# Layer 0 of a hybrid decoder: the first queries, keys and values taken step by step together, with the gates and the norm among the last steps

## The chip, the cores and the metric

One core of one Trainium2 chip runs the whole program. The time is the device time of one execution in microseconds (us); the kernel before has a median of 1263.06 us over three runs. TensorE (PE) does the matrix products, VectorE (DVE) and ScalarE (ACT) the elementwise work, GpSimd (POOL) a part of the weight preparation, and SyncE (SP) issues most of the transfers.

## The reference, cut to what matters

Two layers work on 528 tokens (16 learned ones and 512 real ones) of width 1024. A layer normalises its input, makes one combined projection, runs two groups of heads on it and adds the result back; a gated feed-forward block follows.

```
xn = rmsnorm(h, attn_norm_g)
proj = einsum('bld,dc->blc', xn, w_in)
fq, fk, fv, flog, rq, rk, rv, rg = split(proj)
logf = log_sigmoid(flog + b_fgate)              # 8 forget gates
c = cumsum(logf)                                # along the tokens
logit[t, s] = q_t . k_s / 8 + c[t] - c[s],  s <= t   # 8 attention heads of 64
ret = retention(rotate(rq), rotate(rk), rv)     # 4 retention heads of 128
h = h + concat(attention, silu(rg) * groupnorm(ret)) @ w_out
h = h + (silu(rmsnorm(h) @ w_gate) * (rmsnorm(h) @ w_up)) @ w_down
```

All of it is in float32. After both layers a last norm follows, and the learned tokens are dropped.

## The kernel before, in words

The activations lie transposed: `h[0]` to `h[7]` are eight tiles of 128 features x 528 tokens, and "step k" of a projection is its part for `h[k]`. A product keeps float32 accuracy by splitting both sides into a high and a low part of a faster type: `xh`, `xl` of the activations (ACT at L309 makes the high part, DVE at L310 the low one), `whi`, `wlo` of the weights (ACT at L180, then DVE or POOL at L183). A step of a projection to 128 columns is three products on two halves of 264 tokens each, so six matmuls at L207. The norm's factor per token, `R`, is not applied to the input: it multiplies what comes out of PSUM.

The projections are numbered jobs. Job 0 makes the queries of the first pair of attention heads, job 1 its keys, job 2 its values; jobs 3 to 6 make value, query, key and gate of the first retention head. `fetch` gives a job one of three `raw` buffers and loads 512 KB of weights; `convert` splits them. The split parts go into a ring of two pairs `whi`, `wlo`, but job 2 has a place of its own, the tile `ptl`, which later holds attention weights. A job's accumulator is one of two double banks `psd`; job 2 uses two of the four single banks `psa`, which also serve the gates, the norm, the scores and the transposes.

PE runs in the order in which the plan in `layer` is written. The other engines' queues are ordered at build time by a scheduler with priorities, except where `pin` keeps the written order, and each queue is worked through strictly in order on the chip. In layer 0 the plan before is: queries and keys alternating step by step (16 steps), then the gates (64 small matmuls at L376, `forget_gates`), the sums of squares (L385, `forget_sums`), half of the values (4 steps), the spreading of the norm factor over all partitions (L419, `spread_norm`, with ACT copies at L421 that make `R`), the other half of the values, and the rotary tables (`ropes`, L1289, each scaled by `R`).

`squares` (ACT L321 and L326, added up by DVE at L333 in the tile `ss`) must be done before the sums. From the sums a chain of small operations on `z` (L390 to L400) makes the norm factor `r` (ready after L394) and the logarithms of the gates (ready after L400). `forget_scan` runs four scans over them (L410) and writes the result to DRAM (`cdr`, L412); each head reads it back, copied to all partitions (`bc`, L517). `q_done` (L451, L457, L458), `k_done` (L464, L471, L472) and `v_done` (L478) take the projections out of PSUM; in layer 0 the first two are held back in a list and called by `first`. The scores of the first head pair (L528) follow among the retention steps; DVE at L534 and L535 adds the mask and `bc`, finds the smallest value `nmax` and thereby frees the `psa` bank, in which later scores or transposes (L438) can then be put.

At the start the weights of jobs 0 and 1 are loaded in three pieces each (step 0 and 1, step 2 and 3, step 4 to 7) between the tiles of `h`. The tile with the gates' weights `wf` and the pattern `pick`, with which `spread_norm` multiplies, is `pth`.

Of the kernel before, what the change touches and what calls it, by code (L numbers as in the profile page):

```python
# [10 lines left out]
F32 = mybir.dt.float32  # L11
# [5 lines left out]
NK = D // 128  # L17
# [4 lines left out]
FH = 8  # L22
# [18 lines left out]
def hybrid_kernel(ctx, tc, x_t, w_in, w_fl, w_out, w_gate, w_up, w_down, vecs, b_fg, rope, decay, mask, ident, out_t):  # L41
# [97 lines left out]
    def fetch(j):  # L139
        job = jobs[j]  # L140
        if "load" in job:
            job["load"]()
        elif "raw" not in job:
            n = job["src"].shape[1]
            job["raw"] = wp.tile([128, NK, 128], F32, name="raw", tag="raw", bufs=3)
            if j > 1:
                nc.sync.dma_start(job["raw"], job["src"]) if n == NK else \
                    nc.sync.dma_start(job["raw"][:, 0:n], job["src"])
# [5 lines left out]
    def convert(j, upto=NK, pinned=False):  # L154
# [18 lines left out]
        while job["split"] < min(n, upto):  # L173
            c0 = job["split"]
            c1 = min(n, c0 + (2 if j < 2 and c0 < 4 else 4))
            size, hi, lo = job["w"][c0 // job["w"][0][0]]
# [9 lines left out]
    def dense_steps(src, parts, pool=False, banks=False, ahead=(1, 4), own=None, wait=None):  # L186
# [6 lines left out]
        def chunk(k0, k, n, xs, cols, ps, done):  # L193
            def go():
# [8 lines left out]
                xh, xl = xs(k)  # L203
                order = ((hi, xh), (lo, xh), (hi, xl)) if j < 2 and k == 0 else ((hi, xh), (hi, xl), (lo, xh))
                for i, (w, x) in enumerate(order):
# [149 lines left out]
    def gate_weights(l, st):  # L355
        t = at("pth", F32, (128, NK + 16, 32))
        nc.gpsimd.memset(t, 0.0)
        st["wf"], st["pick"] = t[:, 0:NK], t[:, NK:].rearrange("p (j a) b -> p j (a b)", j=4)
        for j in range(4):
            nc.gpsimd.memset(st["pick"][32 * j:32 * j + 1, j], 1.0)  # L360
        g = V_ATTN + l * NK
        with tc.high_priority():
            nc.vector.tensor_mul(t[:, 0:NK, 0:FH], st["wfr"], vec[:, g:g + NK].unsqueeze(2).broadcast_to([128, NK, FH]))

# [77 lines left out]
    def fox_dense(l, g, ly, real, st):  # L442
# [38 lines left out]

        def own():
            t = at("ptl", shape=(128, 2, NK, 128))
            return t[:, 0], t[:, 1]

        return [dense_steps(w_in[l, 3 * g + i], [(0, lambda k: ly["x"][k], NK, c, f)], g > 0 or (i == 2 and not first), i == 2,
                            ((), (6, 6))[i] if first and i < 2 else (1, 4), own if first and i == 2 else None, ly["wait"] if g == 0 and i < 2 - l else None)
                for i, (c, f) in enumerate(((QC, q_done), (FULL, k_done), (FULL, v_done)))]
# [788 lines left out]
    def layer(l):  # L1277
# [25 lines left out]
        def start():  # L1303
            if l == 0:

                idle = psum_a()
                for _ in range(8):
                    nc.tensor.matmul(idle, ones, wide, start=True, stop=True)
                def piece(queue, c0, c1):
                    for j in range(2):  # L1310
                        fetch(j)
                        queue.dma_start(jobs[j]["raw"][:, c0:c1], jobs[j]["src"][:, c0:c1])

                for j in range(2):
                    fetch(j)
                    nc.scalar.dma_start(jobs[j]["raw"][:, 0:2], jobs[j]["src"][:, 0:2])
                    if j == 0:
                        nc.scalar.dma_start(vec, vecs)
                nc.scalar.preload_act_table_set(LOGS)
                for k in range(NK):  # L1320
                    nc.sync.dma_start(h[k], x_t[k])
# [5 lines left out]
                def parts(k):  # L1327
                    for j in range(2):
                        convert(j, upto[k], True)
# [13 lines left out]
        q, k, v = fd(0)  # L1343
        qk = [f for pair in zip(q, k) for f in pair]
        gates = [lambda: forget_gates(l, ly)]
# [9 lines left out]
        if l == 0:  # L1355
            plan += qk + [first_parts] + gates + sums + v[:4] + norm + first + scan + first + v[4:] + [ropes]
        else:
# [105 lines left out]
```

## Time and profile before

| what | value |
|---|---|
| median of 3 runs | 1263.06 us (1262.17 to 1263.28) |
| profiled execution | 1261.7 us, of which the span of instructions 1259.9 us |
| mean granted TensorE clock | 0.999 |
| PE busy | 1249.5 us (99% of the span) |
| DVE, ACT, POOL busy | 992.2, 683.0, 264.8 us |
| first matmul of job 0, first of job 3 | 5.31 us, 27.48 us |
| start of layer 1's queries | 640.11 us |

A row of a timeline gives start, length, engine, line, operation, the tile written, the tiles read, the shape and the count; in square brackets is the idle time of the engine before it and what ended that. Lengths of matmuls overlap, so the distance between starts is what one costs. A row of the chain of waits gives start, length and what held the end at that time. A row of waits gives the engine and its line, what it waited for, the total in us, how many times and the longest.

### The profile page before, as it was taken

The page shows a single profiled execution, that of the slowest core. Times are in us where ns is not written, and L with a number is a line of the kernel's source. Part 1 is how long each engine was busy: PE and PEld are TensorE (multiplying, and loading weights), DVE is VectorE, ACT ScalarE, POOL GpSimd, SP SyncE. Part 2 cuts the span into 40 slices and gives each one's busy share as a digit, 9 for nine tenths or more (in the row PEclk, how much of TensorE's full clock was granted, in tenths as well). Part 3 has the DMA queues.
Part 4 walks back from the last instruction along what each step waited for, and adds up shares of the span by engine and source line. Part 5 has one row for each costly group of instructions (what it writes and reads, how often), then busy time and mean ns, then how long its engine had stood idle before and what let it go on. Part 6 is the DMA issues. An engine that isn't in the chain of part 4 may idle for free.

```text
span 1259.9 us, 23793 instructions
## 1 busy us (share of the span) xinstructions
PE 1249.5 (99%) x9360; PEld 1192.6 (95%) x9360; DVE 992.2 (79%) x1851; ACT 683.0 (54%) x1239; POOL 264.8 (21%) x534
## 2 busy tenths in 40 slices
PE   9999999999999999999999999999999999999997
PEld 8999999999999999999999988998889999999996
DVE  8877856779888888887776777567899888888867
ACT  7666555776444444444455665457764444444445
POOL 3455645510000000000035545554100000000000
PEclk9999999999999999999999999999999999999999
DMA  7322223123333333332323222222323333333321
GB/s 237 86 76 90 80 77 93 51 74 124 93 98 101 99 101 101 101 101 84 102 77 118 76 94 78 90 78 67 109 86 124 101 101 101 101 101 101 100 84 68
DMA packets 45808, 120.58 MB, mean 96 GB/s; under 512 B 5488, under 2 KB 12400, under 8 KB 45696
## 3 DMA queue, kind: packets, MB, share of 16 engines
q1 hardware_dynamic: 45264, 118.77, 30.2%
q8 instruction: 73, 1.20, 0.4%
q14 instruction: 39, 0.32, 0.1%
q10 hardware_dynamic: 432, 0.29, 0.1%
HBM read 116.91 MB, written 2.13 MB: 94 GB/s over the span
## 4 chain that ended last, share of the span: by engine, by line
PE 98%; DVE 1%; DMA 1%; ACT 0%; SPq 0%; issue 0%; DVEq 0%
PE psd L207 32%; PE psa L933 19%; PE psd L1068 14%; PE psd L933 13%; PE psa L207 5%; PE psa L1068 4%; PE psa L438 2%; PE psa L615 2%; PE psa L528 2%; PE psa L782 1%; PE psa L752 1%; DMA h<-x_t 0%; PE psa L280 0%; PE psa L624 0%; PE psa L376 0%; DMA raw<-w_in 0%
## 5 line engine op out<-in xcount | busy, mean ns | idle before, releaser
L183 POOL TENSOR_TENSOR wlo<-raw,whi 128x128 fp32r<-128x128 f32 x504 | 259.4, 549 | 261.9 <-ACT whi L180 259.4
L207 PE MATMUL psd<-xh,whi 128*128 128x264 f32 (+1 forms) x792 | 195.6, 314 | 0.3 <-ACT xh L309 0.3
L207 PE MATMUL psd<-xh,wlo 128*128 128x264 f32 (+1 forms) x792 | 186.3, 303 | 0.0
L207 PE MATMUL psd<-xl,whi 128*128 128x264 f32 (+1 forms) x792 | 185.9, 302 | 0.3 <-DVE xl L310 0.3
L207 PEld LDWEIGHTS psd<-xh,whi 128*128 128x128 f32 x792 | 128.0, 189 | 5.3 <-ACT xh L309 0.8
L207 PEld LDWEIGHTS psd<-xh,wlo 128*128 128x128 f32 x792 | 126.8, 188 | 6.0
L207 PEld LDWEIGHTS psd<-xl,whi 128*128 128x128 f32 x792 | 127.3, 188 | 4.7 <-DVE xl L310 0.8
L180 ACT CAST whi<-raw 128x512 fp32r<-128x512 f32 (+1 forms) x167 | 98.1, 614 | 56.0 <-PE psd L207 37.9
L921 ACT CAST whi<-raw 128x1024 fp32r<-128x1024 f32 (+2 forms) x62 | 54.9, 885 | 53.0 <-PE psd L933 38.8
L921 ACT CAST fwhi<-raw 128x1024 fp32r<-128x1024 f32 (+2 forms) x62 | 55.6, 897 | 47.1 <-PE psd L933 39.6
L85 POOL MEMSET kl<- 64x528 f32 x2 | 1.1, 534 | 345.5 <-PE psa L933 345.4
L922 DVE TENSOR_TENSOR wlo<-raw,whi 128x1024 fp32r<-128x1024 f32 (+2 forms) x62 | 62.9, 1015 | 11.2 <-ACT whi L921 11.0
L922 DVE TENSOR_TENSOR fwlo<-raw,fwhi 128x1024 fp32r<-128x1024 f32 (+2 forms) x62 | 64.0, 1032 | 8.6 <-ACT fwhi L921 8.4
L933 PE MATMUL psa<-th,whi 128*128 128x264 f32 (+1 forms) x232 | 65.4, 282 | 0.0
L933 PE MATMUL psa<-th,wlo 128*128 128x264 f32 (+1 forms) x232 | 65.4, 282 | 0.0
L933 PE MATMUL psa<-tl,whi 128*128 128x264 f32 (+1 forms) x232 | 65.3, 282 | 0.0
L933 PE MATMUL psa<-th,fwhi 128*128 128x264 f32 (+1 forms) x224 | 63.4, 283 | 0.0
L933 PE MATMUL psa<-tl,fwhi 128*128 128x264 f32 (+1 forms) x224 | 63.3, 283 | 0.0
L933 PE MATMUL psa<-th,fwlo 128*128 128x264 f32 (+1 forms) x224 | 63.3, 282 | 0.0
L548 ACT ACTIVATE pd<-pd,nmax 128x144 f32<-128x144 f32 (+1 forms) x64 | 36.9, 576 | 42.0 <-DVE nmax L535 27.4
L921 ACT CAST fwhi<-S 128x1024 fp32r<-128x1024 f32 x20 | 21.0, 1050 | 70.3 <-PE psa L933 66.5
L999 ACT COPY e<-psa 128x264 f32<-128x264 f32 (+1 forms) x114 | 42.9, 376 | 28.3 <-PE psa L933 24.0
(352 smaller groups left out, 4008.3 us busy)
## 6 DMA issues: line engine op xcount, KB each, us to landing
raw<-w_in SPq DMA_DIRECT2D x54, 512.0 KB, 3.5
raw<-w_gate SPq DMA_DIRECT2D x44, 512.0 KB, 3.9
fraw<-w_up SPq DMA_DIRECT2D x38, 512.0 KB, 3.7
raw<-w_down SPq DMA_DIRECT2D x64, 256.0 KB, 2.8
raw<-w_out SPq DMA_DIRECT2D x16, 512.0 KB, 3.5
raw<-w_down SPq DMA_DIRECT2D x32, 192.0 KB, 2.5
bc<-cdr SPq DMA_DIRECT2D x16, 264.0 KB, 3.6
raw<-w_up SPq DMA_DIRECT2D x6, 512.0 KB, 3.4
```

Source lines behind the costliest of these rows:

```text
L180: pin((nc.vector.tensor_copy if j + c0 == 0 else nc.scalar.copy)(hi, job["raw"][:, c0:c1]), pinned)
L183: pin(sub(lo[:, i:i + wide], job["raw"][:, c0 + i:c0 + i + wide], hi[:, i:i + wide].bitcast(F32)), pinned)
L207: nc.tensor.matmul(ps[1][b][:, 0:c1 - c0], w[:, wk, :], x[:, c0:c1], start=(k == 0 and i == 0), stop=(k == n - 1 and i == 2))
L438: nc.tensor.transpose(ps[:, 128 * j:128 * j + 128], src[:, o:o + 128], idt)
L528: nc.tensor.matmul(sc[0:nq, 0:c1 - c0], st["q"][s][:, q0:q0 + nq], kk[:, c0:c1], start=(i == 0), stop=(i == 1))
L548: nc.scalar.activation(pr, pr, AF.Exp, bias=nmax[0:nq], scale=-1.0, accum_out=rsum)
L615: nc.tensor.matmul(po[:, c0:SEQ], v[:, j, :], pp[:, j, META + c0:T], start=(j == 0 and i == 0), stop=(j == 4 and i == 1))
L921: nc.scalar.copy(hi, src)
L922: nc.vector.tensor_sub(lo, src, hi.bitcast(F32))
L933: nc.tensor.matmul(bank()[:, 0:b.shape[-1]], a[:, o + k, :], b, start=(fresh and k == 0 and i == 0), stop=(k == n - 1 and i == 2), skip_gr ...
L999: nc.scalar.copy(self.t["e"][:, i], self.t["x"][:, 0:w])
L1068: nc.tensor.matmul(v[:, 0:c1 - c0], a[:, s * n + k, :], b[:, c0:c1], start=(k == 0 and i == 0), stop=(k == n - 1 and i == 2))
```

## The change

Layer 0 now takes queries, keys and values together: step k of all three jobs before step k+1 of any. Gates and sums come after the sixth step (k = 5), the spreading of the norm after the seventh, the scan's instructions are written behind the eighth step of queries and keys, and the `done` functions are called where their last step ends, since the list that held them back is used in layer 1 alone. Job 2's weights are loaded and converted in three pieces as well, on SP; the first tile of `h` is issued ahead of the pieces. Job 1 gets the tile `pth` as its own place and job 2 keeps `ptl`, so jobs 3 and 4 are the first to use the second and again the first pair of the ring. `wf` and `pick` move from `pth` to the tiles `d` and `gr`, which later hold decay tables and a gate, in both layers. Nothing is left out of the computation and nothing is added to it.

```diff
@@ fetch, convert, dense_steps
-            if j > 1:
+            if j > 2:
                 nc.sync.dma_start(job["raw"], job["src"]) if n == NK else \
...
-            c1 = min(n, c0 + (2 if j < 2 and c0 < 4 else 4))
+            c1 = min(n, c0 + (2 if j < 3 and c0 < 4 else 4))
...
-                order = ((hi, xh), (lo, xh), (hi, xl)) if j < 2 and k == 0 else ((hi, xh), (hi, xl), (lo, xh))
+                order = ((hi, xh), (lo, xh), (hi, xl)) if j < 3 and k == 0 else ((hi, xh), (hi, xl), (lo, xh))
@@ gate_weights
-        t = at("pth", F32, (128, NK + 16, 32))
+        t = at("d", F32, (128, T), 2)[:, 0:32 * NK].rearrange("p (k c) -> p k c", k=NK)
+        u = at("gr", F32)[:, 0:512].rearrange("p (j q) -> p j q", j=4)
         nc.gpsimd.memset(t, 0.0)
-        st["wf"], st["pick"] = t[:, 0:NK], t[:, NK:].rearrange("p (j a) b -> p j (a b)", j=4)
+        nc.gpsimd.memset(u, 0.0)
+        st["wf"], st["pick"] = t, u
@@ fox_dense
-        def own():
-            t = at("ptl", shape=(128, 2, NK, 128))
+        def own(tag):
+            t = at(tag, shape=(128, 2, NK, 128))
             return t[:, 0], t[:, 1]
 
         return [dense_steps(w_in[l, 3 * g + i], [(0, lambda k: ly["x"][k], NK, c, f)], g > 0 or (i == 2 and not first), i == 2,
-                            ((), (6, 6))[i] if first and i < 2 else (1, 4), own if first and i == 2 else None, ly["wait"] if g == 0 and i < 2 - l else None)
+                            () if first else (1, 4), (lambda i=i: own(("pth", "ptl")[i - 1])) if first and i else None, ly["wait"] if l and g + i == 0 else None)
@@ layer
+                nc.sync.dma_start(h[0], x_t[0])
                 def piece(queue, c0, c1):
-                    for j in range(2):
+                    for j in range(3):
...
-                for j in range(2):
+                for j in range(3):
                     fetch(j)
-                    nc.scalar.dma_start(jobs[j]["raw"][:, 0:2], jobs[j]["src"][:, 0:2])
+                    (nc.scalar if j < 2 else nc.sync).dma_start(jobs[j]["raw"][:, 0:2], jobs[j]["src"][:, 0:2])
...
-                for k in range(NK):
+                for k in range(1, NK):
                     nc.sync.dma_start(h[k], x_t[k])
...
-                    for j in range(2):
+                    for j in range(3):
                         convert(j, upto[k], True)
...
-        qk = [f for pair in zip(q, k) for f in pair]
...
-            plan += qk + [first_parts] + gates + sums + v[:4] + norm + first + scan + first + v[4:] + [ropes]
+            for i in range(NK):
+                plan += [q[i], k[i]] + (scan if i == NK - 1 else []) + [v[i]]
+                if i == 5:
+                    plan += [first_parts] + gates + sums
+                elif i == 6:
+                    plan += norm
+            plan += [ropes]
```

What this does to the queues is shown at three places. Names end in the buffer's number where one is kept; a number behind x counts equal instructions in a row.

PE before, from the sums of squares to the first step of the retention values (job 3, `psd`, `whi`); `ptl` marks the values' weights:

```order
L385 MATMUL psa<-ss,ones 32x132 x4
L385 MATMUL psa<-sq,ones 32x132 x4
L207 MATMUL psa<-xh_157,ptl 128x264 x2
...
L207 MATMUL psa<-xh_177,ptl 128x264 x2
L419 MATMUL psa<-z,pth 128x132 x4
L207 MATMUL psa<-xh_185,ptl 128x264 x2
...
L207 MATMUL psa<-xh_197,ptl 128x264 x2
L207 MATMUL psd<-xh_157,whi 128x264 x2
```

And now, where `pth` marks the keys' weights and the spreading is at L421:

```order
L387 MATMUL psa<-ss,ones 32x132 x4
L387 MATMUL psa<-sq,ones 32x132 x4
L207 MATMUL psd<-xh_203,whi 128x264 x2
...
L207 MATMUL psa<-xh_203,ptl 128x264 x2
L421 MATMUL psa<-z,gr 128x132 x4
L207 MATMUL psd<-xh_207,whi 128x264 x2
...
L207 MATMUL psa<-xh_207,ptl 128x264 x2
L207 MATMUL psd<-xh_161,whi 128x264 x2
```

Before, four steps stood between sums and spreading and four between spreading and job 3. Now three stand at either place, and those behind the spreading are the last ones of queries, keys and values.

DVE before, from the end of the gates' chain to the low parts of the keys; `z_449<-z` is a scan, `tq` the queries or keys out of PSUM, `cr` a rotary table:

```order
L400 TENSOR_TENSOR z<-z 128x132
L451 SCALAR_TENSOR_TENSOR tq<-psd,R 128x528
L410 SCALAR_TENSOR_TENSOR z_449<-z 8x132
L464 SCALAR_TENSOR_TENSOR tq<-psd,R 128x528
L410 SCALAR_TENSOR_TENSOR z_449<-z,z_449 8x132
L458 TENSOR_TENSOR qs_443<-tq,qs_443 64x528
L410 SCALAR_TENSOR_TENSOR z_449<-z,z_449 8x132
L458 TENSOR_TENSOR qs_446<-tq,qs_446 64x528
L410 SCALAR_TENSOR_TENSOR z_449<-z,z_449 8x132
L472 TENSOR_TENSOR kl_99<-tq,kh_460 64x528
L472 TENSOR_TENSOR kl_100<-tq,kh_464 64x528
```

And now:

```order
L402 TENSOR_TENSOR z<-z 128x132
L1291 SCALAR_TENSOR_TENSOR cr<-cr,R 128x528
L453 SCALAR_TENSOR_TENSOR tq<-psd,R 128x528
L466 SCALAR_TENSOR_TENSOR tq<-psd,R 128x528
L412 SCALAR_TENSOR_TENSOR z_482<-z 8x132
L460 TENSOR_TENSOR qs_460<-tq,qs_460 64x528
L412 SCALAR_TENSOR_TENSOR z_482<-z,z_482 8x132
L460 TENSOR_TENSOR qs_463<-tq,qs_463 64x528
L412 SCALAR_TENSOR_TENSOR z_482<-z,z_482 8x132
L474 TENSOR_TENSOR kl_99<-tq,kh_474 64x528
L412 SCALAR_TENSOR_TENSOR z_482<-z,z_482 8x132
L474 TENSOR_TENSOR kl_100<-tq,kh_478 64x528
```

The first rotary table has come ahead of the queries, and the fourth scan behind one of the two low parts of the keys.

SP at the start now, with the semaphores that a row waits for (`DMAHW` ones count transfers that have landed, eight at a time):

```order
L1311 DMA h_73<-x_t 128x528
L1325 DMA h_74<-x_t 128x528
L1320 DMA raw<-w_in 128x256
L1316 DMA raw<-w_in 128x256 x2
L1316 DMA raw<-w_in 128x256 [waits DMAHW0_49]
L1325 DMA h_75<-x_t 128x528 [waits DMAHW1_49]
L1325 DMA h_76<-x_t 128x528 [waits DMAHW2_49]
L1316 DMA raw<-w_in 128x512 [waits DMAHW3_49]
L1316 DMA raw<-w_in 128x512 [waits DMAHW4_49]
L1316 DMA raw<-w_in 128x512 [waits DMAHW5_49]
L1325 DMA h_77<-x_t 128x528 [waits DMAHW6_49]
```

Three pieces of the values' weights stand ahead of `h[4]` (`h_77`); before, those were one load behind `h[7]`, and `h[2]` (`h_75`) was issued without a wait.

More of the change, by code (lines that the diff above doesn't have):

```diff
@@ L362, in gate_weights @@
         with tc.high_priority():
-            nc.vector.tensor_mul(t[:, 0:NK, 0:FH], st["wfr"], vec[:, g:g + NK].unsqueeze(2).broadcast_to([128, NK, FH]))
+            nc.vector.tensor_mul(t[:, :, 0:FH], st["wfr"], vec[:, g:g + NK].unsqueeze(2).broadcast_to([128, NK, FH]))
     def quarter(j):
```

## The prediction

> **What bounds the kernel now.** I read the page's busy times first, then PE's waits over the whole span.
>
> ```profile
> PE 1249.5 (99%) x9360; PEld 1192.6 (95%) x9360; DVE 992.2 (79%) x1851; ACT 683.0 (54%) x1239; POOL 264.8 (21%) x534
> ...
> PE psa L1308 <- DVE wide L61: 1.6, 1, 1.6
> PE psa L752 <- DVE nmax L535: 0.4, 1, 0.4
> PE psd L207 <- DVE xl L310: 0.3, 1, 0.3
> PE psd L207 <- ACT xh L309: 0.3, 1, 0.3
> ```
>
> PE works nearly all the time, and all its listed waits are 2.6 us, of which 1.6 lie before any data is there. The change keeps every matmul, so it can win only what PE stands still in the first 28 us, and it loses wherever a step that was covered is covered no longer. Next, the chain of waits of the start and PE's timeline.
>
> ```profile
> 4.84 0.44 SPq L1312
> 5.32 5.53 DMA h<-x_t
> 10.87 0.75 ACT xh L309
> 11.65 0.78 DVE xl L310
> 12.47 5.87 PE psd L207 x46
> ```
>
> ```profile
> 5.31 0.51 PE L207 MATMUL psd<-xh,whi 128*128 128x264 f32 x2 [0.26 <-ACT xh L309]
> ...
> 6.46 0.40 PE L207 MATMUL psd<-xh,whi 128*128 128x264 f32 x2
> ...
> 11.67 0.51 PE L207 MATMUL psd<-xh,whi 128*128 128x264 f32 x2
> 12.47 0.51 PE L207 MATMUL psd<-xl,whi 128*128 128x264 f32 x2 [0.29 <-DVE xl L310]
> 12.82 0.41 PE L207 MATMUL psd<-xh,wlo 128*128 128x264 f32 x2
> ...
> 17.93 0.41 PE L207 MATMUL psd<-xh,wlo 128*128 128x264 f32 x2
> 18.27 2.01 PE L376 MATMUL psa<-h,pth 128*32 128x132 f32 x64
> ...
> 20.09 0.41 PE L385 MATMUL psa<-ss,ones 128*32 128x132 f32 x8
> 20.32 0.41 PE L385 MATMUL psa<-sq,ones 128*32 128x132 f32 x8
> 20.66 0.51 PE L207 MATMUL psa<-xh,ptl 128*128 128x264 f32 x2
> ...
> 23.68 1.06 PE L419 MATMUL psa<-z,pth 128*128 128x132 f32 x8
> 24.50 0.49 PE L207 MATMUL psa<-xh,ptl 128*128 128x264 f32 x2
> ...
> 27.48 0.40 PE L207 MATMUL psd<-xh,whi 128*128 128x264 f32 x2
> ...
> 36.38 0.29 PE L528 MATMUL psa<-kh,qs 128*128 128x272 f32 x1
> ```
>
> From 12.82 to 17.93 lie 21 pairs of matmuls: 0.243 us a pair, 0.73 a step of one projection. The first three pairs take 1.15 (5.31 to 6.46), 0.42 too much, waiting for the first tile's parts. At the fifth step two pairs take 1.15 (11.67 to 12.82) and the pair ahead of them 0.1 too long, 0.77 lost together: `h[4]`, issued at 5.32, landed at 10.85. That is the stall that this change can reach.
>
> Last, DVE's and ACT's timelines and SP's behind the sums, because the first scores hang on them.
>
> ```profile
> 19.25 0.71 DVE L333 TENSOR_TENSOR ss<-ss,sq 128x528 f32<-128x528 f32 x1 [0.52 <-ACT ptl L180]
> ...
> 22.66 0.45 DVE L394 SCALAR_TENSOR_TENSOR z<-z 128x132 f32<-128x132 f32 x1
> ...
> 24.70 0.56 DVE L400 TENSOR_TENSOR z<-z 128x132 f32<-128x132 f32 x1 [0.35 <-ACT z L399]
> 25.24 0.71 DVE L451 SCALAR_TENSOR_TENSOR tq<-psd,R 128x528 f32<-128x528 f32 x1
> ...
> 29.78 0.48 DVE L410 TENSOR_TENSOR_SCAN z<-z,z 8x132 f32<-8x132 f32 x1
> 30.29 1.44 DVE L472 TENSOR_TENSOR kl<-tq,kh 64x528 fp32r<-64x528 f32 x2
> ...
> 32.45 0.70 DVE L1289 SCALAR_TENSOR_TENSOR cr<-cr,R 128x528 f32<-128x528 f32 x1
> ...
> 35.14 0.17 DVE L535 CUSTOM_DVE_ANT_0 pm<-psa,bc 16x16 f32<-16x16 f32 x1 [0.68 <-DMA bc<-cdr]
> ```
>
> ```profile
> 24.57 0.64 ACT L421 COPY R<-psa 128x264 f32<-128x264 f32 x2
> ```
>
> ```profile
> 30.29 0.35 SPq L412 DMA_DIRECT2D cdr<-z  x1
> 31.80 0.82 SPq L517 DMA_DIRECT2D bc<-cdr  x2
> ```
>
> The last scan ends at 30.26; it goes out to DRAM at 30.29, comes back from 31.80, and DVE can free the first score bank from 35.14 to 35.31. PE wants a bank for the third scores at 36.38. So this chain is ahead of PE by only 1.07 us, and no wait shows.
>
> **The change part by part.** S is the start of the last sums (20.32 before); distances from S are what carries over.
>
> *Three jobs a step.* PE now needs a new tile of `h` only every 3 x 0.73 = 2.19 us, not every 1.46. `h[4]` is wanted at 5.31 + 0.42 + 12 x 0.73 = 14.5; even if it lands 1.3 us later than 10.85, its parts take 0.75 and 0.78 and are there. So the 0.77 goes; the 0.42 stays, as the first products and what they wait for are the same. The gates stand behind 18 single steps, 54 pairs: 5.31 + 0.42 + 54 x 0.243 = 18.85, and 0.1 for the change of kind as before (17.93 + 0.24 to 18.27) gives 18.95. That is 0.68 *later* than 18.27, because two more steps (1.46) stand ahead and only 0.77 is won. S becomes 21.00.
>
> *Without new waits*, PE would reach job 3 at 18.95 + 2.39 (18.27 to 20.66) + 2.19 + 0.82 (23.68 to 24.50) + 2.19 = 26.54, not 27.48: a gain of 0.94. Three waits eat it.
>
> *The sums* begin 0.23 ahead of S (20.09) and need the last add, which ended at 19.25 + 0.71 = 19.96, just in time. The squares that it adds stand on ACT, now behind the casts of the values' weights too:
>
> ```profile
> L180 ACT CAST whi<-raw 128x512 fp32r<-128x512 f32 x8 | 4.7, 616 | 4.8 <-issue 3.5 <-DMA raw<-w_in 1.3
> L180 ACT CAST whi<-raw 128x256 fp32r<-128x256 f32 x3 | 1.1, 400 | 0.1
> L183 DVE TENSOR_TENSOR ptl<-raw,ptl 128x512 fp32r<-128x512 f32 x2 | 1.8, 948 | 0.0
> L183 DVE TENSOR_TENSOR wlo<-raw,whi 128x512 fp32r<-128x512 f32 x2 | 1.4, 692 | 0.9 <-ACT whi L180 0.9
> ```
>
> The casts, two small and one large, are 2 x 0.40 + 0.62 = 1.42 us. PE comes at 21.00 - 0.23 = 20.77. If ACT has no slack, the last add ends at 21.38 and PE waits 0.61; if the 1.3 us for which ACT waited for weights take the casts in, it waits nothing. I take 0.25, nearer to the slack that the rows show.
>
> *The spreading* needs `r`, ready at 22.66 + 0.45, S + 2.79. PE comes 0.34 + 2.19 = 2.53 behind S: 0.26 of waiting.
>
> *Job 3 needs a `psd` bank*, freed by DVE's `tq` for the queries. Before, `tq` started at S + 4.92, directly behind L400 and `R` (25.21). Now the rotary table stands ahead of it, 0.65 of distance (0.70 busy): start S + 5.57, end S + 6.28. PE comes at S + 2.79 + 0.82 + 2.19 = S + 5.80 and waits 0.5. Job 3 starts at S + 6.33 = 27.33 at best: of the 0.94, 0.15 is left.
>
> *The third scores.* From `tq` to the end of the last scan DVE needed 30.26 - 25.24 = 5.02; one low part of the keys (1.44 / 2 = 0.72) now lies in between, so the scan ends at S + 5.57 + 5.74 = S + 11.31. The way over DRAM to the freed bank is 35.31 - 30.26 = 5.05. PE can go on at S + 16.36 = 37.36; it came at 27.33 + 8.90 (27.48 to 36.38) = 36.23 and waits 1.1. DVE's queue stands behind that instruction: the next mask, the low parts of the turned values and so the release of every other `psa` bank.
>
> *Sum.* The freed bank comes later by 0.68 (gates) + 0.25 (adds) + 0.65 (table) + 0.72 (keys' low part) = 2.30, less the 1.07 by which it was early: +1.23. From there PE has the same work in the same order as before, so nothing gives this back. The profiled 1261.7 (1259.9 span and 1.8 around it) becomes 1262.9; it lies 1.4 under the median of 1263.06, against which the forecast is 1264.3.
>
> The Trainium skill (SBUF — State Buffer, section "SBUF: two separate sides") says that a VectorE operation with two SBUF inputs and a GpSimd operation that reads SBUF lock each other out for a whole instruction. The trace agrees in kind: the values' low parts, run while POOL worked, took 948 ns against 692 for the same shape. By that rule the last one or two adds, which now reach into POOL's work on job 3, would each be longer by some 0.26, and the sum would be +1.5 to +1.75 in place of +1.23.
>
> *Costed at nothing.* The values' low parts move from behind the adds to DVE's gaps at the start. Job 4's weights wait for the ring until the last query step, but are wanted a whole job (8 x 0.73 = 5.8) later; without that cover ACT's 2 x 0.62 would show. The gates' weights in other tiles: in layer 1 they must be there when PE comes, shown by these rows.
>
> ```profile
> 644.95 1.94 PE psa L376 x64
> ...
> L363 DVE TENSOR_TENSOR pth<-wfr,vec x1: 219/219/219, 642.3 to 642.3; 128x64 f32<-128x64 f32 x1
> ```
>
> They are ready 2.4 us early there. On SP, `cdr` stands behind a weight load that waits for POOL's work on job 4; should that end later than the last scan, it adds directly.
>
> **The rivals.**
>
> *The cover suffices.* If the scans finish early enough (DVE's gaps taken differently, the way over DRAM shorter by over 1 us), the third scores don't wait, and only job 3's start counts: -0.9 without any wait, +0.1 with all three. That is 1262.2 to 1263.2. For it speaks that the way over DRAM is mostly transfer time; against it that DVE's order is fixed and the two operations put ahead of the scan's end cost 1.37, more than the 1.07.
>
> *Late data, slower.* Three more pieces stand on SP ahead of `h[4]` at 0.44 each, 1.3 us, and `h[2]` now waits for a landing. If the last tile reaches ACT 1.3 later on top of the 1.42, the last add ends at 19.96 + 2.72 = 22.68, PE waits 1.9 at the sums in place of 0.25, and all behind moves: +2.9, 1266.0. It decides from the point where the last add ends behind 22.3. For it: in the chain this transfer was the one that held the end. Against: PE now draws data at two thirds of the rate, and ACT idled 1.3.
>
> *Much faster*, over 2.5 us, would need more standing still than PE has in the waits.
>
> **How the numbers follow.** What the measurement can tell from no change is some 0.2%, 2.5 us. Forecast (third scores wait, +0.7 to +2.0): 0.65. Cover suffices: 0.18. Late data: 0.14, of which 0.11 beyond 2.5 us. A stall in layer 1 or an unknown one: 0.03, slower by 2.5 in most of it. Of the 0.18, 0.02 goes to a gain beyond 2.5 us from something the waits don't show. So faster 0.02, same 0.84 (0.65 + 0.16 + 0.03), slower 0.14 (0.11 + 0.03). The range leaves out a tenth at either end: 1262.3 (cover suffices with some waiting) to 1266.2 (late data).
>
> **What would show it.** Right: no gap at the fifth step; gates near 18.95; a wait of PE for `tq` near 27; `cdr` issued near 32.3; a wait of PE for `nmax` of about 1.1 us near 36 to 37.4, and layer 1's queries about 1.2 us later than 640.11. Wrong: no wait at the third scores, `cdr` before 31, or gates before 18.3 or behind 20. A wait of over 1 us for `ss` would mean the late data.

## The result and the profile after

The changed kernel takes 1267.08 us (median of 8 runs, 1264.37 to 1267.73); the kernel before, timed beside it, 1262.78 us (8 runs, 1262.01 to 1263.83). The ratio is 1.0029 with a 95% interval of 1.0020 to 1.0038: slower by about 4 us. The profiled execution took 1267.41 us (span 1265.6), 5.7 more than the one of before, so it shows a little more than the median loss. The eight times are not spread evenly: two lie at 1264.4 and 1264.8, six from 1266.4 to 1267.7.

All of the loss arises in the first 45 us. The gates of layer 1, whose row is a good milepost, start at 650.62 us and not at 644.88 (+5.74), and the span ends 5.7 later. The row before, then the row after:

```profile
644.88 2.01 PE L376 MATMUL psa<-h,pth 128*32 128x132 f32 x64
650.62 2.01 PE L378 MATMUL psa<-h,d 128*32 128x132 f32 x64
```

First the waits of PE in the first 50 us of the changed kernel: engine and line, what it waited for, total, how often, longest.

```profile
PE psa L530 <- DVE nmax L537: 2.2, 1, 2.2
PE psa L1310 <- DVE wide L61: 1.6, 1, 1.6
PE psd L207 <- ACT xh L309: 0.7, 1, 0.7
```

The fifth step has no row: the stall of the kernel before is gone. But the first product waits 0.70 for `xh` (0.26 before), and the third scores wait 2.2 us for `nmax`, where the kernel before waited nothing. Together 2.6 us more standing still, less than half of 5.7. The rest is in the distances of PE's timeline:

```profile
1.60 3.78 PE L1310 MATMUL psa<-wide,ones 128*128 128x512 f32 x8 [1.60 <-DVE wide L61]
6.08 0.81 PE L207 MATMUL psd<-xh,whi 128*128 128x264 f32 x2 [0.70 <-ACT xh L309]
6.69 0.64 PE L207 MATMUL psd<-xh,wlo 128*128 128x264 f32 x2
7.13 0.64 PE L207 MATMUL psd<-xl,whi 128*128 128x264 f32 x2
...
10.21 0.64 PE L207 MATMUL psd<-xh,whi 128*128 128x264 f32 x2
10.65 0.49 PE L207 MATMUL psd<-xl,whi 128*128 128x264 f32 x2
...
21.60 2.01 PE L378 MATMUL psa<-h,d 128*32 128x132 f32 x64
23.42 0.41 PE L387 MATMUL psa<-ss,ones 128*32 128x132 f32 x8
23.65 0.41 PE L387 MATMUL psa<-sq,ones 128*32 128x132 f32 x8
...
29.41 0.48 PE L207 MATMUL psd<-xh,whi 128*128 128x264 f32 x2
...
40.76 0.40 PE L530 MATMUL psa<-kh,qs 128*128 128x272 f32 x1 [2.20 <-DVE nmax L537]
...
41.67 0.64 PE L207 MATMUL psd<-xh,wlo 128*128 128x264 f32 x2
42.11 0.64 PE L207 MATMUL psd<-xh,whi 128*128 128x264 f32 x2
...
45.31 0.40 PE L207 MATMUL psd<-xl,whi 128*128 128x264 f32 x2
```

A pair of matmuls normally costs 0.243 us. From 6.69 to 10.65 pairs start 0.44 apart, with no wait between them: the first ten take 4.57 us (6.08 to 10.65) and not 2.43. The same pace comes back after the standstill at the third scores, from 41.67 to 44.97. There the granted clock says what it is. The first fence is the changed kernel, the second the one before (columns: window, its length, busy time and count of PE, PEld, DVE, ACT, POOL, then PEclk, DMA share, GB/s):

```profile
8.00:9.00 1.00, 1.00 (x6) 1.00 (x6) 1.00 (x4) 0.55 (x2) 0.00 (x0) 1.00 0.98 302
...
38.00:41.30 3.30, 1.10 (x9) 0.89 (x8) 0.76 (x6) 0.70 (x4) 1.78 (x5) 1.00 0.71 178
41.40:44.70 3.30, 3.30 (x17) 3.19 (x16) 1.81 (x10) 1.31 (x8) 0.00 (x0) 0.52 0.38 144
44.80:47.00 2.20, 2.20 (x20) 2.20 (x19) 1.88 (x6) 0.44 (x1) 0.00 (x0) 0.97 0.03 7
```

```profile
8.00:9.00 1.00, 1.00 (x11) 1.00 (x9) 1.00 (x2) 0.26 (x1) 0.00 (x0) 1.00 0.91 289
...
41.40:44.70 3.30, 3.30 (x30) 3.27 (x30) 3.04 (x12) 3.19 (x8) 1.93 (x4) 1.00 0.32 72
```

For 3.4 us the clock is half. At the start the column reads 1.00 (first row) although only 6 matmuls fall into that us, where the kernel before has 11, and the pairs have the same distance of 0.44; there the distances decide. (The trace's list of clock records begins only with a step to full clock, in the changed kernel at 10.80 us, and the column counts the time ahead of the list as 1.00.) PE counts as busy throughout, which is why a busy share of 99% hides it.

Last, the chain that the third scores wait for, on DVE (first fence) and SP (second):

```profile
18.46 3.22 DVE L333 TENSOR_TENSOR ss<-ss,sq 128x528 f32<-128x528 f32 x4 [0.52 <-ACT sq L326]
...
25.61 0.30 DVE L396 SCALAR_TENSOR_TENSOR z<-z 128x132 f32<-128x132 f32 x1
...
27.93 0.71 DVE L1291 SCALAR_TENSOR_TENSOR cr<-cr,R 128x528 f32<-128x528 f32 x1
28.55 0.70 DVE L453 SCALAR_TENSOR_TENSOR tq<-psd,R 128x528 f32<-128x528 f32 x1
...
33.91 0.48 DVE L412 TENSOR_TENSOR_SCAN z<-z,z 8x132 f32<-8x132 f32 x1
...
40.54 0.16 DVE L537 CUSTOM_DVE_ANT_0 pm<-psa,bc 16x16 f32<-16x16 f32 x1 [3.09 <-DMA bc<-cdr]
```

```profile
33.35 0.33 SPq L147 DMA_DIRECT2D raw<-w_in  x1
34.42 0.35 SPq L414 DMA_DIRECT2D cdr<-z  x1
37.08 0.82 SPq L519 DMA_DIRECT2D bc<-cdr  x2
```

From the issue of `cdr` to that of `bc`, which waits for its landing, 2.66 us pass; before it were 1.51. A weight load of 512 KB was issued 1.07 us ahead of `cdr`; before, none was.

So three things were to be explained: the half rate at the start, the wait of 2.2 us, and the half rate behind it.

### The profile page after: what moved, and what is told of

It is laid out like the page before. It is cut to its first block, busy times and chain, and to the rows that moved or that the text cites. A ratio compares the mean times of both kernels' runs of the same rounds, so it can differ in the third digit from the quotient of the medians.

```text
span 1265.6 us, 23807 instructions
## 1 busy us (share of the span) xinstructions
PE 1252.8 (99%) x9360; PEld 1196.4 (95%) x9360; DVE 989.8 (78%) x1852; ACT 682.9 (54%) x1240; POOL 265.2 (21%) x536
## 4 chain that ended last, share of the span: by engine, by line
PE 97%; DVE 1%; DMA 1%; ACT 0%; issue 0%; DVEq 0%; ACTq 0%; SPq 0%
PE psd L207 32%; PE psa L935 19%; PE psd L1070 14%; PE psd L935 13%; PE psa L207 5%; PE psa L1070 4%; PE psa L440 2%; PE psa L617 2%; PE psa L530 2%; PE psa L784 1%; PE psa L754 1%; PE psa L280 0%; PE psa L626 0%; DMA vec<-vecs 0%; PE psa L378 0%; DMA bc<-cdr 0%
## 5 line engine op out<-in xcount | busy, mean ns | idle before, releaser
L207 PE MATMUL psd<-xl,whi 128*128 128x264 f32 (+1 forms) x776 | 183.2, 303 | 0.0
```

What stands on the lines that cost most here:

```text
L207: nc.tensor.matmul(ps[1][b][:, 0:c1 - c0], w[:, wk, :], x[:, c0:c1], start=(k == 0 and i == 0), stop=(k == n - 1 and i == 2))
```

## The experiments

The runs' main numbers, all from their profiles but for the last column. "Full clock from" is the first record in the trace's list of clock records, a step to full clock; the pairs of PE's rows reach 0.24 at the same place. S is the start of the last sums; the two columns behind it are the distance from the weight load to `cdr` and from `cdr` to `bc`; then the wait of the third scores, the start of layer 1's gates, and the median. (e6 and e10 leave out seven eighths of one job's weights.)

| run | first product | standstill ahead | full clock from | S | load to `cdr` | `cdr` to `bc` | wait | layer 1's gates | median |
|---|---|---|---|---|---|---|---|---|---|
| before | 5.31 | 0.26 | 4.53 | 20.32 | none | 1.51 | 0 | 644.88 | 1262.78 |
| after | 6.08 | 0.70 | 10.80 | 23.65 | 1.07 | 2.66 | 2.20 | 650.62 | 1267.08 |
| e1 | 5.55 | 0.17 | 7.00 | 22.05 | 1.53 | 2.30 | 1.82 | 647.55 | 1264.38 (one) |
| e2 | 6.03 | 1.15 | 4.67 | 20.73 | none | 1.57 | 0 | 645.25 | 1263.34 |
| e3 | 6.04 | none | 7.66 | 22.19 | 1.53 | 2.14 | 1.74 | 647.55 | 1264.70 |
| e4 | 6.04 | 0.66 | 10.34 | 23.42 | 1.08 | 2.48 | 2.14 | 650.37 | 1266.78 |
| e5 | 5.32 | none | 5.99 | 21.90 | 1.53 | 2.12 | 1.71 | 647.23 | 1265.81 |
| e6 | 5.18 | none | 5.66 | 22.00 | 64 KB | 1.55 | 1.53 | 647.12 | 1263.93 (one) |
| e7 | 6.04 | 0.65 | 5.34 | 22.84 | 1.54 | 2.36 | elsewhere | 652.43 | 1269.96 |
| e8 | 5.43 | 0.42 | 4.45 | 19.94 | none | 1.55 | 0 | 644.85 | 1261.67 |
| e9 | 5.18 | none | 7.10 | 21.51 | 1.07 | 2.62 | 0.30 | 646.89 | 1264.78 |
| e10 | 5.54 | 0.15 | 6.38 | 21.99 | 64 KB | 1.54 | under 0.15 | 646.30 | 1263.64 |
| e11 | 5.35 | none | 6.66 | 20.23 | none | 1.49 | 0 | 644.76 | 1261.78 |
| e12 | 6.03 | none | 6.62 | 22.16 | 1.08 | 2.69 | 0.7 | 647.90 | 1264.60 |

In every profile the warm-up matmuls run at the slow pace too, up to the step to full clock: their 512 columns take 0.43 us, by the column the same as the 0.44 of a pair with 528 (in the changed kernel the fifth starts at 3.47 and the eighth at 4.75).

### The start: e1, e2, e3

**e1**, no edit: a second profile of the changed kernel.

> The changed kernel once more, for its second profile. Theory: the vectors' transfer lands late because of the change (a third job's first piece of 128 KB stands in the transfers beside it), so the first matmul of job 0 again comes near 6.08 us and not near 5.31, and after a standstill of TensorE of about 0.7 us pairs of matmuls again start 0.44 us apart, not 0.243, for 4 to 5 us; gates near 21.6. Rival (that landing was chance): first matmul near 5.3 to 5.4, pairs 0.243 apart from the start, gates near 19.0, time near 1264.5 us.

```profile
5.55 0.81 PE L207 MATMUL psd<-xh,whi 128*128 128x264 f32 x2 [0.17 <-ACT xh L309]
6.15 0.64 PE L207 MATMUL psd<-xh,wlo 128*128 128x264 f32 x2
6.59 0.59 PE L207 MATMUL psd<-xl,whi 128*128 128x264 f32 x2
7.02 0.65 PE L207 MATMUL psd<-xh,pth 128*128 128x264 f32 x4
```

PE's timeline shows neither picture: the first product comes at 5.55, three pairs (not ten) are slow, the gates come at 19.60, and the execution took 1264.38 us. So the vectors' landing varies. ACT's first `xh`, which waits for them, starts at 5.29, 4.76, 5.17, 5.26, 5.25, 4.32 and 4.34 in after, e1, e3, e4, e7, e6 and e12, and at 4.52 and 5.25 in before and e2, where the change is absent. That the change delays them isn't shown; both kernels have early and late landings.

**e2**, the kernel before with one warm-up matmul fewer.

```diff
-                for _ in range(8):
+                for _ in range(7):
```

> The kernel before with 7 warm-up matmuls for 8, nothing else: TensorE then stands still for about 0.7 us ahead of its first product and not 0.26. Theory (TensorE falls to half its rate when it stands still at that place): pairs 0.44 us apart for 4 to 5 us, gates about 1.9 later than 18.27 where transfers don't bound it, time 1264.0 to 1264.8 us. Rival (the slow pairs come from the change itself, as the third job's pieces or its tiles): first matmul still at 5.31, pairs 0.243 apart, time 1262.8 us, no change to the kernel before.

```profile
1.60 3.28 PE L1308 MATMUL psa<-wide,ones 128*128 128x512 f32 x7 [1.60 <-DVE wide L61]
6.03 0.51 PE L207 MATMUL psd<-xh,whi 128*128 128x264 f32 x2 [1.15 <-ACT xh L309]
6.38 0.40 PE L207 MATMUL psd<-xh,wlo 128*128 128x264 f32 x2
```

PE stood still 1.15 us, longer than in the changed kernel, and went on at full pace; the step to full clock, at 4.67, lay ahead of the standstill (4.88 to 6.03). Median 1263.34, ratio 1.0003 (0.9994 to 1.0013). "A standstill here halves the rate" falls in that form. e7 says the same of the changed kernel: 0.65 us of standstill, full pace at once, with the step at 5.34, ahead of it.

**e3**, the changed kernel with 10 warm-up matmuls, so that they reach to the first product.

```diff
-                for _ in range(8):
+                for _ in range(10):
```

> The changed kernel with 10 warm-up matmuls for 8: they end near 6.3 us, so TensorE doesn't stand still ahead of its first product, which comes some 0.25 us later. Theory (half rate after a standstill): pairs 0.243 us apart from the start, gates at 19.7 to 20.0 and not 21.60, time 1.6 to 1.9 us below the changed kernel's 1267.1, so 1265.2 to 1265.5. Rival (the slow pairs come from the third job's pieces): pairs still 0.44 apart to about 10.7, gates near 21.8, time 1267.1 to 1267.4.

```profile
1.60 4.64 PE L1310 MATMUL psa<-wide,ones 128*128 128x512 f32 x10 [1.60 <-DVE wide L61]
6.04 0.73 PE L207 MATMUL psd<-xh,whi 128*128 128x264 f32 x2
...
7.01 0.64 PE L207 MATMUL psd<-xl,whi 128*128 128x264 f32 x2
7.45 0.75 PE L207 MATMUL psd<-xh,pth 128*128 128x264 f32 x4
```

Median 1264.70 (ratio 1.0018, 1.0009 to 1.0028), 2.4 less than the changed kernel; gates at 20.14. The gain is larger than expected, but the pairs were not at full pace from the start: it began at 7.66.

The clock records say what decides it. The steps within one trace lie whole multiples of 3.413 us apart (in after 10.80, 41.52 and 44.94; 41.52 - 10.80 = 30.72 = 9 x 3.413), and where this grid lies differs from execution to execution. Laid over PE's rows it gives one account of all fourteen profiles: the first step up comes at the end of the first 3.41 us of the grid in which PE stood still for no more than 0.57 us. Such a stretch held 0.48 of standstill in before and 0.57 in e8, and the clock rose; it held 0.66 in e4, 0.70 in after and 0.77 in e3 (the time ahead of the first warm-up matmul), and the clock did not. In after the gap of 0.70 lay whole in the stretch from 3.98 to 7.39, so the step came one stretch later, at 10.80. This is read off the profiles afterwards; no run moved the grid.

The Trainium skill (TensorE: Matmul & The Clock Gate, Part 1, "The HAM clock gate") describes this: half the clock until a window of about 3.4 us was busy, with windows that run freely and don't begin with the kernel. The traces agree: the column reads 0.52 and 0.50 where the pace is slow (0.44 a pair for 0.243), the moment varies between executions, and the later stretches last 3.41 us (after) or twice that (e7, below).

### The way through DRAM: e4, e6

**e4**: `cdr` by ACT's queue, away from the weight load on SP's.

```diff
-            nc.sync.dma_start(st["cdr"], z2)
+            (nc.sync if l else nc.scalar).dma_start(st["cdr"], z2)
```

> The changed kernel, with layer 0's scanned sums sent to DRAM by ScalarE's queue and not SyncE's, where they stand behind a weight load of 512 KB that was issued 1.07 us before. Theory (that load holds them up in the queue): from their issue to that of the first transfer that reads them 1.5 us and not 2.66, the third scores wait about 1.0 us for the minimum and not 2.2, time 1.1 us lower, and up to 2.1 lower if the shorter standstill leaves TensorE at full rate behind it: 1265.0 to 1266.0. Rival (it isn't the place in the queue but the load's use of the same transfer engines): still about 2.6 us, wait 2.2, time 1267.1.

`cdr` was issued at 34.19 on ACT, `bc` at 36.67: 2.48 us, the wait 2.14, the median 1266.78 (ratio 1.0028, 1.0017 to 1.0039). Another queue brings no more than 0.2 us, and nothing in the time: the place in SP's queue is not the cause.

**e6**: the load itself cut to an eighth.

```diff
+                if j == 7:
+                    n = 1
+                    nc.gpsimd.memset(job["raw"][:, 1:], 0.0)
...
-                    nc.sync.dma_start(job["raw"][:, 0:n], job["src"])
+                    nc.sync.dma_start(job["raw"][:, 0:n], job["src"][:, 0:n])
```

> The changed kernel with the 512 KB weight load that SyncE issues 1.07 us before the scanned sums cut to 64 KB (the rest of that job's weights is set to zero by GpSimd, so one projection of layer 0 is computed with an eighth of its weights). Theory (that load's bytes fill the transfer engines when the scanned sums are sent): from the sums' issue to that of the first transfer that reads them 1.5 to 1.6 us, as in the kernel before, not 2.3 to 2.7, and the third scores wait some 0.8 to 1.1 us less than the 1.8 to 2.2 of the changed kernel's two profiles. Rival (the write to DRAM itself takes longer in this place): still 2.1 us or more.

```profile
31.89 0.33 SPq L151 DMA_DIRECT2D raw<-w_in  x1
33.42 0.35 SPq L417 DMA_DIRECT2D cdr<-z  x1
34.97 0.96 SPq L522 DMA_DIRECT2D bc<-cdr  x2
```

With its bytes gone, `cdr` to `bc` is 1.55, as before. The table bears it out: without the load 1.49 to 1.57, 1.5 us behind it 2.12 to 2.36, 1.1 us behind it 2.48 to 2.69. The wait, though, fell by 0.2 to 0.3 only (1.53 against 1.71 to 1.82 in e1, e3 and e5), not by the 0.8 expected: from `bc`'s issue to DVE's first use of it 3.65 us passed (34.97 to 38.62) in place of 3.23 in e1 (35.77 to 39.00). Why the second transfer took longer here stays open; in e10, with the same cut, it took 3.24. So the load's price is shown for the first transfer; of its price for the wait I have only 0.2 to 0.3. For the whole time it is the difference of e10 and e9 (below), which differ by this cut alone: some 1.1 us in the median.

### The vectors first: e5, e8, e11

One edit, in the changed kernel (e5) and in the one before (e8, and e11 in more rounds):

```diff
+                    if j == 0:
+                        nc.scalar.dma_start(vec, vecs)
                     (nc.scalar if j < 2 else nc.sync).dma_start(jobs[j]["raw"][:, 0:2], jobs[j]["src"][:, 0:2])
-                    if j == 0:
-                        nc.scalar.dma_start(vec, vecs)
```

> The changed kernel with the vectors (vec, 24 KB) issued first on ScalarE's queue, ahead of the first weight piece and not behind it. Theory (they land late because the pieces issued before and beside them hold them up, by chance more or less): they land by 4.2 us, the first matmul of job 0 comes at 5.0 to 5.4 in place of 5.55 to 6.08, TensorE hardly stands still behind the warm-up matmuls, pairs reach 0.243 us by 8.5 at the latest, time 1264.0 to 1265.0 us; the wait of the third scores, 1.8 us or more, stays. Rival (their place in the queue doesn't matter, only how much is under way on the transfer engines): still 4.7 to 5.2, first matmul up to 6.1, time as the changed kernel's 1267.1.

> The kernel before with the same edit as the one that puts the vectors first. Theory (the late vectors cost the kernel before little, since its first steps wait for pieces of x and of the weights anyway): 1262.0 to 1262.8 us, within 0.5 of the kernel before. Rival (the start weighs on both alike): 0.7 us or more below it, 1261.8 or less.

> The kernel before with the vectors first, once more and in more rounds, for the size of its gain: 1261.4 to 1262.0 us against 1262.5 to 1262.8 of the kernel before, if the first run's 0.9991 was no chance; 1262.3 or more if it was.

In e5 the first `xh` starts at 3.82, and the first product at 5.32 with no gap behind the warm-up matmuls, as expected. In all five runs with the vectors first (e5, e8 to e11) `xh` starts at 3.67 to 3.91, in the nine others at 4.32 to 5.29: their place in the queue matters. The median of 1265.81 (1263.94 to 1266.29; ratio 1.0023, 1.0013 to 1.0033) misses the 1264 to 1265: two of nine executions lie at 1263.9, five at 1265.8 or more. A good start alone doesn't remove the long times; the standstill at the third scores is still there.

In the kernel before, the edit gives 1261.67 (ratio 0.9991, 0.9982 to 1.0000) and 1261.78 (0.9993, 0.9984 to 1.0002), against 1262.77 and 1262.99 beside them. The rival was nearer, with gains of 1.1 and 1.2 us. It is the fastest version of this study, though both intervals just reach "no change".

### The standstill at the third scores: e7, e9, e10, e12

**e7**: the scores three steps later.

```diff
-            m0, r0, places = (((7, 31), (34, 40.5), ...
+            m0, r0, places = (((10, 31), (34, 40.5), ...
```

> The changed kernel with the scores and transposes of the first heads of layer 0 and 1 spread from step 10 and not from step 7, so that three more steps of 0.73 us stand on TensorE ahead of them. Theory (the loss beside the start is one standstill of TensorE of about 2 us at the third scores, and the half rate of 3.4 us that follows it in some executions): no wait for the minimum over 0.3 us, granted clock 1.00 at 41 to 45 us, time 1.7 to 3 us lower, 1264.0 to 1265.4. Rival (the work behind the scores is late all the same, so the standstill moves to their transposes or to the products with v): a wait of 1.5 to 2 us stands at another tile before 60 us, time 1267.

Its waits of PE in the first 80 us, and the clock around them:

```profile
PE psa L440 <- DVE nmax L537: 1.7, 2, 1.2
PE psa L530 <- DVE sq L723: 1.7, 1, 1.7
```

```profile
40.00:42.80 2.80, 1.50 (x11) 1.27 (x11) 1.23 (x9) 1.47 (x7) 0.00 (x0) 1.00 0.55 195
42.90:49.60 6.70, 5.03 (x22) 4.94 (x22) 4.69 (x16) 3.07 (x8) 0.38 (x1) 0.50 0.01 2
49.70:52.00 2.30, 2.30 (x21) 2.30 (x21) 1.74 (x7) 1.90 (x5) 1.53 (x4) 1.00 0.00 0
```

1269.96 us (ratio 1.0059, 1.0044 to 1.0074). The rival holds: the standstill moved to the transposes and to the next scores, grew to 3.4 us, and the half clock lasted 6.8 us. A late chain isn't cured by putting its user later when other users of the same banks follow.

**e9**: the vectors first, and the scans called behind the norm. **e10**: the same and the small load. **e12**: ten warm-up matmuls and the early scans, the vectors in their place.

```diff
-                plan += [q[i], k[i]] + (scan if i == NK - 1 else []) + [v[i]]
+                plan += [q[i], k[i], v[i]]
...
-                    plan += norm
+                    plan += norm + scan
```

> The changed kernel with the vectors first on ScalarE's queue (as in an earlier run) and the scans of the gates called right behind the norm's spreading, so that two of VectorE's operations of the rotation that stood between and behind the scans come after them. Theory (the third scores' standstill is made of the scans' end and of the way through DRAM that the 512 KB load lengthens): the last scan ends about 1.3 us earlier against the start of the last sums, at S + 10.0 and not S + 11.4; the sums are sent about 0.2 to 1.0 us behind the load and so take 2.5 us or more to the first transfer that reads them, which takes some of it back; the wait for the minimum falls from 1.7 to 0.6 to 1.1 us; the half rate at 41 us goes, times gather at 1262.9 to 1263.9. Rival (the way through DRAM waits for the load however early the scans end): wait 1.5 or more, times as without the scans' move, 1264 to 1266.3.

> As the run with the vectors first and the scans early, and the 512 KB load ahead of the scanned sums cut to 64 KB (one projection of layer 0 is computed with an eighth of its weights, the rest is zero). Theory (with the load's bytes gone, the sums are out at S + 10.0 and read at S + 11.6, the minimum comes 1.4 us earlier than in the run with the small load alone, where TensorE waited 1.5 us): wait 0 to 0.3 us, no half rate behind it in any execution, times close together at 1262.3 to 1263.0, so no more than 0.3 above the kernel before. Rival (something else holds the third scores, as the freed bank or the masked first scores): wait of 0.8 us or more, times 1263.5 or more.

> The changed kernel with 10 warm-up matmuls for 8 and with the scans called right behind the norm's spreading; the vectors stay in their place. Theory (two standstills of TensorE, ahead of the first product and at the third scores, each followed by some us at half rate in some executions, make the spread of the changed kernel's times, 1264.4 to 1267.7): with both closed, the wait for the minimum is under 0.6 us, no clock under 1.00 is granted at 41 us, and the times lie in one group no wider than 1.5 us, at 1263.5 to 1264.6. Rival (the spread has another source, as the transfers' chance landing): again two groups more than 1.5 us apart, or times up to 1266 and more.

PE's waits of e12 between 25 and 60 us, and its clock where the changed kernel had half:

```profile
PE psa L530 <- DVE nmax L537: 0.7, 1, 0.7
PE psd L207 <- DVE tq L453: 0.6, 1, 0.6
PE psa L440 <- DVE vv L506: 0.5, 1, 0.5
```

```profile
41.40:44.70 3.30, 3.17 (x27) 3.20 (x28) 3.27 (x13) 1.91 (x5) 0.00 (x0) 1.00 0.17 66
```

In e9 the wait for `nmax` is 0.30, in e12 0.7, in e10 too small to be listed. The spread is what reacts: e12's eleven times lie between 1264.12 and 1264.93, e9's ten between 1263.82 and 1265.19, without those at 1266 and above, which e3 (three of ten) and e5 still have. That is what the theory of two standstills asked for.

The mean granted clock, on record for every execution, bears it out: 3.41 us at half lower it by 0.0013. In none of 83 executions of the kernel before that were timed beside e1 to e12 is it under 0.998. It is 0.997 or less in five of eight of the changed kernel, five of eight of e4, three of ten of e3 (just the three at 1266.06 to 1266.39, the other seven lie at 1264.72 or below), four of nine of e5 (1265.81 to 1266.16), all four of e7, and none of the 31 of e9, e10 and e12. These counts are lower bounds, since 0.998 can hide such a stretch.

So a standstill of about 1.7 us (e3, e5) has the half clock behind it in some executions, though not in their profiles. The grid accounts for this too. The clock fell where the standstill within one stretch of 3.41 us was 2.20 (after), 2.14 (e4) and 1.71 (e7, in two pieces), and stayed where it was 1.71 (e5), 1.53 (e6), 1.51 (e1, whose 1.82 a grid line cuts) and 0.87 (e3, whose 1.74 is cut in halves).

The level missed the forecasts. e12's median of 1264.60 (ratio 1.0012, 1.0003 to 1.0021) equals the lower part of e3's times: the wait of 1.74 was split into 0.7 for `nmax`, 0.6 for `tq`, which now starts behind a scan, and 0.5 for `vv`, 1.8 in all. The early scans removed the half rate that followed one long standstill (from e5 to e9 and from e3 to e12), not the lateness. e9 came out at 1264.78 (1.0016, 1.0007 to 1.0025), 0.9 above its forecast, and e10 at 1263.64 (1.0006, 0.9997 to 1.0015), 0.6 above. e10 still reaches layer 1's gates 1.42 later than before: its S is 1.67 later, PE waits 0.6 for `tq`, and only some of that is won back by the shorter way to job 3.

## Why the prediction was wrong

It said 1264.3, no change that can be measured, at 0.84; measured are 1267.08 and a loss beyond the 0.2%. In its own order:

*The start: wrong, and the first step that failed.* "The 0.42 stays, as the first products and what they wait for are the same" gave the gates at 5.31 + 0.42 + 54 x 0.243 + 0.1 = 18.95. Profiled: first product +0.77, by the vectors' chance landing; ten pairs at half pace, 4.57 - 2.43 = 2.14 in place of the 0.42, so +1.72; other +0.16. Gates at 21.60. The pace of a matmul was taken as fixed at 0.243 from a profile in which the step to full clock happened to come ahead of the first product (4.53 against 5.31); here it came at 10.80. In the executions where it came early (e1, e5, e6) the gates stood at 19.2 to 19.6, near the forecast.

*The stall at the fifth step goes: right.* No wait is left there.

*The sums' wait, 0.25 (0 to 0.61): right in mechanism and about in size.* None in the profiled run, since PE was late; 0.20, 0.35 and 0.51 in e1, e5 and e6; 0.82 in e7, beyond the 0.61. The last add ended at 21.68 (18.46 + 3.22), short of the 22.3 from which the rival "late data" was to decide. This rival did not come in: the loss has its size, but another cause.

*The spreading's and job 3's waits, 0.26 and 0.5: did not occur in the profiled run.* `r` was ready at S + 2.26 (25.91), not S + 2.79, and `tq` ran from S + 4.90. The chain on `z` was quicker because POOL worked on job 3 up to 24.50 and then stood still until 28.58, where before it worked through from 19.62 to 27.93 (first row before, the others after):

```profile
19.62 8.31 POOL L183 TENSOR_TENSOR wlo<-raw,whi 128x128 fp32r<-128x128 f32 x16 [17.14 <-ACT whi L180]
20.50 4.00 POOL L183 TENSOR_TENSOR wlo<-raw,whi 128x128 fp32r<-128x128 f32 x8 [17.97 <-ACT whi L180]
28.58 1.88 POOL L183 TENSOR_TENSOR wlo<-raw,whi 128x128 fp32r<-128x128 f32 x4 [4.08 <-ACT whi L180]
```

The two operations that read `z` twice from SBUF took 0.30 and 0.29 (L396, L402) where L394 and L400 had taken 0.45 and 0.56; those that read PSUM took 0.30 in both. e1 has both cases in one profile: L396 ran at 24.33, with POOL at work up to 24.62, and took 0.44; L402 ran at 26.49, with POOL standing still, and took 0.30. The rule of the Trainium skill that the prediction weighed (SBUF — State Buffer, "SBUF: two separate sides") is borne out by that, but in the other direction than feared; the last adds lost at most 0.08 to it (784 against 708 ns). Where the scans were called early, job 3 did wait 0.6 for `tq` (e9, e10, e12).

*The scans' end, S + 11.31: right in e1 and e6 (S + 11.39), in part by luck.* In e1 `tq` began 0.23 earlier than forecast (S + 5.34), and from there to the end of the scans 6.05 passed in place of 5.74. The profiled run, with the quick chain, has S + 10.74.

*The way over DRAM, 5.05: mis-sized.* It measured 6.31 (34.39 to 40.70). 1.15 of the 1.26 lie between `cdr` and `bc`, behind the load on SP. The prediction saw that load stand ahead of `cdr`, but priced only its wait for POOL, not its bytes: it was issued in time, and just this put 512 KB on the transfer engines ahead of 16.5 KB that were urgent.

*The third scores' wait, 1.1: right in place, 2.20 in size.* They resumed at 40.76, 3.40 later than the forecast 37.36: S 2.65 later, scans 0.57 nearer to S, the way 1.26 longer, and 0.06 of rounding and smaller steps. (The prediction's 37.36, and its 27.33 for job 3, count from S = 21.00 and so leave out its own 0.25 for the adds, which its sum of +1.23 has; with it the forecast is 37.61.)

*"From there PE has the same work in the same order as before, so nothing gives this back": half right.* The order held, but the work didn't take the same time. From 40.76 on, 5.74 - 4.38 = 1.36 was added up to layer 1 (1.42 in e4), where e1, e3 and e5, with no half clock there, gave back 0.18 to 0.20. So the stretch at half clock cost some 1.6 us. The prediction has no term for what follows a wait.

So the forecast sum describes the executions without the two half-rate stretches: e1 took 1264.38. That the number fits is partly luck, since e1's own sum is another one (a slow start of some 0.8, a way through DRAM 0.67 longer, a wait of 1.8). The median is set by the others: with the first stretch shortened it is 1264.70 (e3), and with the second gone from all executions too 1264.60 (e12), 1.4 above the kernel before and near the forecast's +1.2. What remains open is why `bc` took longer in e6, and in what share of executions the step to full clock comes late, since the mean clock doesn't count the time ahead of it.

## What to carry to other kernels

Before a dense stretch is costed at its steady pace, look at how the same stretch runs in a second profile, and compare distances of starts, not busy shares: an engine that is busy 99% can be at half pace. A wait of about 2 us on TensorE can cost more than itself (here 1.6 us more), so closing it is worth more than its length; splitting it helps where the pieces lie far apart (e12), not where they fall close together (0.47 and 1.24 within 2.4 us in e7). Moving its user later can make it worse. A small transfer on the critical chain should not be issued 1.1 to 1.5 us behind a large one, on the same queue or another.

## What the hardware showed that was not expected

The standstill needed for a fall of the clock is shorter than the 3.4 us that the Trainium skill gives as the limit for gaps (TensorE: Matmul & The Clock Gate, "HAM oscillation — how this bites in real kernels"): 2.14 and 2.20 us at the third scores did it (e4, after). What counted was the part within one 3.41 us of the grid: 1.71 is found on both sides (fallen in e7, not in e5), 1.53 and less did not do it (e6, e1, e3).

A rise of the clock bears less: 0.48 and 0.57 us of standstill in the deciding stretch didn't hinder it (before, e8), 0.66 to 0.77 did (e4, after, e3). So a standstill in the warm-up costs or doesn't cost by where the grid lies: 0.65 and 1.15 us cost nothing behind the step (e7, e2), and 0.66 ahead of it put e4's gates at 21.37, where e7, with its first product at the same 6.04, has 19.76.

16.5 KB sent to DRAM take 1.5 us to the issue of their reader, and 2.1 to 2.7 when 512 KB were issued 1.5 to 1.1 us ahead of them, from another queue as well as from the same.
